# Input projection of the two mixers in groups of up to 512 columns, and the second pair of MLA heads set ahead of the compressed keys

## The chip, the cores and the metric

The kernel runs on one core of one Trainium2 chip. The metric is the device time of one execution in microseconds (us); the median of three runs stands for the kernel. TensorE (PE) multiplies into eight PSUM banks, VectorE (DVE) and ScalarE (ACT) read the banks and work on SBUF, GpSimd (POOL) works on SBUF only, and SyncE (SP) issues the loads of the weights. Each engine works through its own instructions in a fixed order.

## The reference, cut to what matters

The program is two transformer blocks one after the other. The first block has two layers, and in each layer a mixer stands between two feed-forward parts:

```python
for l in range(DEPTH):                                   # DEPTH = 2, T = 256 tokens, D = 1024
    x = x + 0.5 * swiglu(rmsnorm(x, ffn1_norm[l]), ...)
    h = rmsnorm(x, mix_norm[l]) @ w_in[l]                # 1024 -> 2290 columns
    h_a, h_b, h_c = jnp.split(h, [A_COLS, A_COLS + B_COLS], axis=-1)
    o_a = mla_mixer(h_a, ...)                            # 6 heads
    o_b = nsa_mixer(h_b, ...)                            # 6 heads, each with compressed keys and a window
    o_c = diff_mixer(h_c, ...)                           # 4 heads, two score matrices each
    x = x + jnp.concatenate([o_a, o_b, o_c], axis=-1) @ w_out[l]
    x = x + 0.5 * swiglu(rmsnorm(x, ffn2_norm[l]), ...)
```

The change touches the product with `w_in` and the order of the heads after it. The rest of the first block and the whole second block (a convolution and state-space part, then a mixture of experts) stay as they are.

## The kernel before

Weights come from memory in units of 1 MB, 128 rows by 2048 fp32 numbers, in four buffers called `st`. A helper (`split`, lines 154 to 169) splits each unit in two halves: ACT writes the rounded high part `wh` (L166), DVE the rest `wl` (L167), six buffers of each. Every product of the dense parts is three matmuls: high by high, high by low, low by high. All matmuls are issued by one helper (L98), so the tile names tell them apart.

The mixer (`_mixer`) first makes h. Its tile is called `win` in the trace. The stationary operand is the normalized input (`xhl`, 128 rows by 128 tokens), the moving operand the weight columns. Nine groups of 242 or 256 columns are made, each group in one PSUM bank whose two halves hold the two blocks of 128 tokens: 8 pieces of the inner dimension, 2 blocks of tokens and 3 products are 48 matmuls for a group, 432 for a layer. ACT then copies a group out with the norm's factor into `hA` (MLA), `hQ` and `hV` (NSA), `hC` and `hW` (differential heads).

The order of the work is one string, `ORDER`. In it `w` and digits are the groups, `mp`, `np` and `dp` prepare the three kinds of heads, `m0` to `m5`, `n0` to `n5` and `d0` to `d3` are the heads, `df` finishes the differential ones:

```python
ORDER = "w01 w5 w2 mp m0 m1 w8 w3 w4 w6 np w7 dp m2 m3 d0 d1 n0 n1 d2 d3 n2 n3 n4 n5 m4 df m5"
```

A scheduler takes the string as an order of precedence and fills what would be waits with later work that is ready; the order on each engine is then fixed. PSUM tags of the mixer are `S` (3 banks, scores and some preparation), `T` (2, transposes), `O` (1, outputs of head pairs) and `W` (2, projection and the output product).

A head runs like this: scores on PE (`S`), row maxima on DVE (`mx`, L730), exponentials on ACT (`P`, L734), scaling of P by DVE and POOL (L744), transposes of P on PE (`ptp`), copies of them by ACT or DVE (`PT`), and for each pair of heads the product with the values on PE (`opair`), copied out by ACT and DVE (`ohl`).

Compressed keys (`nsa_prepare`, step `np`) are a chain through three engines. PE transposes parts of `hQ` and `hV` (`kvc`, L781 and L782). ACT and DVE copy them in turn into `Z` (L788, four copies). DVE adds the position terms (`blk`, L794, four times). PE multiplies the result by the weights `phi` (`h`, 16 products). ACT and DVE apply the activation, and PE makes the keys and values (`kcmp`, `vcmp`). PE also transposes queries and keys there (`qtb`, `ktb`), and the step `dp` those of the differential heads (`qct`, `kct`).

At the end of the mixer the output product (`wo`) adds 192 matmuls of 256 columns for a layer. It needs the heads' outputs one after another, and its first products are spread among the last heads.

Of the kernel before, what the change touches and what calls it, by code (L numbers as in the profile page):

```python
# [22 lines left out]
KD = 8  # L23
# [13 lines left out]

LOW = {k: "pp" for k in ["b3", "x0", "x1", "x2", "x3"]}
LOW.update({k: "vp" for k in ["h3", "g2"]})
ORDER = "w01 w5 w2 mp m0 m1 w8 w3 w4 w6 np w7 dp m2 m3 d0 d1 n0 n1 d2 d3 n2 n3 n4 n5 m4 df m5"  # L40


class Block:
# [125 lines left out]
            out.append(hl)  # L169
        return out  # L170

    def cols(self, w, *segs):

        wv = w.rearrange("(k p) c -> p k c", p=128)
        out, c = [], 0
        for a, b in segs:
            out.append((c, wv[:, :, a:b]))
            c += b - a
        return self.load(out, wv.shape[1], c)
# [344 lines left out]
    def _mixer(self, l, xops, after):  # L524
        nc, a, ap, tr = self.nc, self.a, self.ap, self.nc.tensor.transpose
        xh, xl, _ = xops
        ident = self.ident
        w_in = a["w_in"][l]
        ACT = lambda o, i, **k: nc.scalar.activation(o, i, AF.Copy, **k)

        def tok(name, n, tag=None, bufs=1):
            return ap.tile([128, 2, n], F32, name=name, tag=tag or name, bufs=bufs)

        hA, hQ, hV, hC, hW = tok("hA", 352), tok("hQ", 768), tok("hV", 402), tok("hC", 512), tok("hW", 256)
        oh, ol, _ = self.pair("ohl")
        B0, C0 = 352, 1522
        q0, kc0, vc0, ks0, vs0, kw0, vw0 = [B0 + c for c in (0, 384, 512, 640, 768, 896, 1024)]
        groups = [
            ([(0, 256)], [(hA, 0, 0, 256)]),
            ([(256, 352), (vw0, C0)], [(hA, 256, 0, 96), (hV, 256, 96, 146)]),  # L540
            ([(q0, q0 + 256)], [(hQ, (0, 3), 0, 192), (hQ, 64, 192, 64)]),
            ([(q0 + 256, vc0)], [(hQ, (192, 2), 0, 128), (hQ, 384, 128, 128)]),
            ([(ks0, vs0), (kw0, vw0)], [(hQ, 512, 0, 256)]),
            ([(vc0, ks0), (vs0, kw0)], [(hV, 0, 0, 256)]),
            ([(C0, C0 + 256)], [(hC, 0, 0, 256)]),
            ([(C0 + 256, C0 + 512)], [(hC, 256, 0, 256)]),
            ([(C0 + 512, C0 + 768)], [(hW, 0, 0, 256)]),
        ]
        units = {}

        def fetch(i):
            if i < len(groups):
                units[i] = self.cols(w_in, *groups[i][0])


        small = {}
# [20 lines left out]

        steps = ORDER.split()
        queue = []
        for step in steps:  # L580
            if step[0] == "w":
                for c in step[1:]:
                    queue.append(lambda i=int(c): units.update({i: self.cols(w_in, *groups[i][0])}))
            elif step == "mp":
                queue.append(fetch_u)
            elif step == "np":
                queue.append(fetch_phi)
# [10 lines left out]
        r = self.inv_rms(pss[:, 0:2], 2)  # L598

        tags = list("WWSS")  # L600

        def w_in_groups(ids):

            ws = [self.split(units[i], "k") for i in ids]
            ps = [self.bank(tags.pop(0) if tags else "W", "win") for _ in ids]
            for k0 in range(KD):
                for k, i, t in ([(k0, i, t) for i in range(len(ids)) for t in range(2)] if len(ids) > 1 else
                                [(k, 0, k0) for k in range(KD)] if k0 < 2 else []):
                    w, p, n = ws[i], ps[i], units[ids[i]][2]
                    o = p[:, t * 256:t * 256 + n]  # L610
                    ts = slice(t * 128, (t + 1) * 128)
                    first = t == 0 and k == 0
                    last = t == 1 and k == KD - 1
                    wh, wl = (v[:, k % 4] for v in w[k // 4])
                    self.mm(o, xh[:, k, ts], wh, first, False)
                    self.mm(o, xh[:, k, ts], wl, False, False)
                    self.mm(o, xl[:, k, ts], wh, False, last)
            for i, p in zip(ids, ps):
                for dst, d, c, m in groups[i][1]:
                    for t in range(2):  # L620
                        src = p[:, t * 256 + c:t * 256 + c + m]
                        if isinstance(d, tuple):

                            o = dst[:, t, 0:384].rearrange("p (u c) -> p u c", c=64)[:, d[0] // 64::2][:, 0:d[1]]
                            src = src.rearrange("p (u c) -> p u c", c=64)
                        else:
                            o = dst[:, t, d:d + m]
                        ACT(o, src, scale=r[:, t:t + 1])


        def mla_prepare():
# [114 lines left out]
        C0, C1 = slice(256, 384), slice(0, 256)  # L746
# [141 lines left out]
        def diff_prepare():  # L888
            for t in range(2):
                self.rope(hC[:, t].rearrange("p (h c) -> p h c", h=16)[:, :, 0:8]  # L890
                          .rearrange("p h (i f) -> p h i f", i=2), 16, 4, t)
            qC = ap.tile([128, 2, T], F32, name="qC", tag="qC")

            kC = [ap.tile([128, 4, T], F32, name="kC", tag=tag) for tag in ("kC0", "hC")]
            for k in kC:
                nc.gpsimd.memset(k, 0.0)
            p, p2 = self.bank("T", "qct"), self.bank("S", "kct")
            for c in range(2):
                for t in range(2):
# [55 lines left out]
        for step in steps:  # L955
            if step == "mp":
                mla = mla_prepare()
                fetch()
            elif step == "np":
                nsa = nsa_prepare()  # L960
                fetch()
            elif step == "dp":
                dif = diff_prepare()
            elif step == "df":
                diff_finish()
            elif step[0] == "w":
                w_in_groups([int(c) for c in step[1:]])
                for _ in step[1:]:
                    fetch()
            else:  # L970
                {"m": mla_head, "n": nsa_head, "d": diff_head}[step[0]](int(step[1]))
# [4 lines left out]
        for b in range(4):  # L976
            for j, (wh, wl) in enumerate(self.split(wo[b], "n")):
                p = self.bank("WS"[j], "wo")
# [940 lines left out]
```

## Time and profile before

| | |
|---|---|
| three runs | 1525.80, 1527.27, 1530.02 us (median 1527.27) |
| the profiled execution | 1530.64 us, its span 1528.6 us |
| busy: PE, DVE, ACT, POOL | 98%, 67%, 48%, 6% |
| mean granted TensorE clock | 0.993 |
| first layer's mixer, from its first `win` to the next `gu` on PE | 200.07 to 340.07 us |

The profile page gives shares of the whole span. What a change in the mixer is worth has to be read in the mixer's own stretches, since the engine that ends last is not the same in each. Where a timeline is shown, a row is one instruction or a run of like ones: start, duration, engine, line, operation, tiles, sizes, count, and in brackets how long the engine sat idle before it and for what. Starts on PE are given by the trace, ends are modelled, so the pace of PE is read from start to start. An fp32 matmul of the heads shows as two records; the projection's matmuls show as one.

### The profile page before, as it was taken

The numbers are of one execution on the slowest core, as the hardware profiler recorded it, in microseconds if no ns is written. First come the engines' busy times: TensorE is split into PE (matmuls) and PEld (weight loads), VectorE is DVE, ScalarE is ACT, GpSimd is POOL, SyncE is SP. The second block draws the span as 40 slices with busy tenths as digits, with TensorE's granted clock in tenths as the row PEclk, the third lists the DMA queues.
The fourth block names the chain that finished last, engine by engine and source line by source line (L and its number), as shares of the span: only waits on it lengthen the run. The fifth ranks groups of instructions, "written<-read, shape, count | busy, mean of one in ns | idle before, by whom it ended". The sixth has DMA issues, their size and how long they took to land.

```text
span 1528.6 us, 25294 instructions
## 1 busy us (share of the span) xinstructions
PE 1490.9 (98%) x9906; PEld 1252.3 (82%) x9906; DVE 1025.6 (67%) x2016; ACT 728.5 (48%) x1382; POOL 91.8 (6%) x142
## 2 busy tenths in 40 slices
PE   8999999999999999999999999999899999999996
PEld 7999998789999989999888999999799987344432
DVE  6787775868677787777577877779888875122112
ACT  6555565755455555555665655547554442001011
POOL 0000000520000000000015000000510100000000
PEclk9999999999999999999999999999999999999998
DMA  7756664116556565656530555666444578999992
GB/s 252 255 165 193 192 165 157 62 61 216 188 174 193 175 189 186 193 193 175 170 119 2 193 187 175 192 191 207 148 130 124 188 294 330 371 392 392 392 395 108
DMA packets 223559, 308.93 MB, mean 202 GB/s; under 512 B 20908, under 2 KB 167608, under 8 KB 223432
## 3 DMA queue, kind: packets, MB, share of 16 engines
q1 hardware_dynamic: 223128, 306.71, 60.2%
q8 instruction: 80, 1.31, 0.4%
q10 hardware_dynamic: 304, 0.53, 0.1%
q14 instruction: 47, 0.39, 0.1%
HBM read 306.16 MB, written 1.05 MB: 201 GB/s over the span
## 4 chain that ended last, share of the span: by engine, by line
PE 92%; DVE 5%; ACT 2%; issue 1%; DMA 0%; POOL 0%; ACTq 0%; DVEq 0%
PE gu L98 32%; PE acc L98 16%; PE proj L98 7%; PE win L98 6%; PE gate L98 4%; PE y L98 4%; PE up L98 4%; PE h L98 3%; PE wo L98 3%; PE S L98 2%; PE moe L98 1%; PE opair L98 1%; PE zp L98 1%; PE xgp L98 1%; PE ptp L696 1%; DVE wl L167 1%
## 5 line engine op out<-in xcount | busy, mean ns | idle before, releaser
L167 DVE TENSOR_TENSOR wl<-st,wh 128x1024 fp32r<-128x1024 f32 (+1 forms) x370 | 446.9, 1219 | 201.9 <-ACT wh L166 190.7
L166 ACT ACTIVATE wh<-st 128x1024 fp32r<-128x1024 f32 (+1 forms) x382 | 399.5, 1059 | 338.4 <-PE gu L98 134.6
L98 PE MATMUL gu<-xhl,wh 128*128 128x512 f32 (+1 forms) x1440 | 486.6, 391 | 3.1 <-ACT wh L166 2.2
L98 PE MATMUL gu<-xhl,wl 128*128 128x256 f32 x1408 | 381.7, 280 | 0.0
L98 PEld LDWEIGHTS gu<-xhl,wh 128*128 128x128 f32 x1440 | 267.1, 189 | 60.9 <-ACT wh L166 2.6
L98 PEld LDWEIGHTS gu<-xhl,wl 128*128 128x128 f32 x1408 | 260.7, 189 | 0.2
L98 PE MATMUL acc<-hx,wh 128*128 128x256 f32 x1408 | 252.3, 281 | 0.0
L98 PEld LDWEIGHTS acc<-hx,wh 128*128 128x128 f32 x1408 | 216.3, 188 | 1.7
L98 PE MATMUL acc<-hx,wl 128*128 128x256 f32 x704 | 196.7, 281 | 0.0
L98 PEld LDWEIGHTS acc<-hx,wl 128*128 128x128 f32 x704 | 132.6, 188 | 0.0
L98 PE MATMUL proj<-uhl,wh 128*128 128x272 f32 (+2 forms) x592 | 127.5, 306 | 4.7 <-DVE dv L1186 1.6
L98 PE MATMUL win<-wh,xhl 128*128 128x256 f32 (+1 forms) x576 | 109.9, 286 | 0.2 <-DVE xT L410 0.2
L98 PEld LDWEIGHTS proj<-uhl,wh 128*128 128x128 f32 x592 | 95.8, 191 | 9.7 <-ACT cv L1224 1.7
L98 PE MATMUL proj<-uhl,wl 128*128 128x272 f32 (+2 forms) x328 | 95.0, 290 | 0.0
L98 PEld LDWEIGHTS win<-wh,xhl 128*128 128x128 f32 x576 | 91.0, 191 | 3.8 <-issue 3.1
L98 PE MATMUL win<-wl,xhl 128*128 128x256 f32 (+1 forms) x288 | 81.9, 284 | 0.0
L394 ACT ACTIVATE hx<-up 128x512 fp32r<-128x512 f32 x44 | 27.7, 630 | 87.2 <-DVE up L393 87.2
L98 PEld LDWEIGHTS proj<-uhl,wl 128*128 128x128 f32 x328 | 62.4, 190 | 0.2
L734 ACT ACTIVATE P<-S,mx 128x256 f32<-128x256 f32 (+2 forms) x128 | 49.0, 404 | 19.0 <-DVE mx L730 4.5
L744 POOL TENSOR_SCALAR P<-P,mx 128x128 f32<-128x128 f32 (+2 forms) x88 | 53.9, 632 | 58.6 <-DVE mx L737 42.7
L1816 DVE SCALAR_TENSOR_TENSOR ys<-y,rc,ys 128x512 fp32r<-128x512 f32 x16 | 11.7, 748 | 67.0 <-ACT ys L1636 66.6
L98 PEld LDWEIGHTS win<-wl,xhl 128*128 128x128 f32 x288 | 54.9, 191 | 0.6 <-issue 0.3
(524 smaller groups left out, 2117.8 us busy)
## 6 DMA issues: line engine op xcount, KB each, us to landing
st<-ffn_wg SPq DMA_DIRECT2D x44, 1024.0 KB, 6.0
st<-ffn_wu SPq DMA_DIRECT2D x44, 1024.0 KB, 5.4
st<-ffn_wd SPq DMA_DIRECT2D x44, 1024.0 KB, 4.8
st<-w_in SPq DMA_DIRECT2D x36, 1024.0 KB, 5.4
st<-w_out SPq DMA_DIRECT2D x16, 1024.0 KB
mf<-expert_w_gate SPq DMA_DIRECT2D x25, 512.0 KB, 9.4
mf<-expert_w_down SPq DMA_DIRECT2D x21, 512.0 KB, 10.7
mf<-expert_w_up SPq DMA_DIRECT2D x18, 512.0 KB, 11.0
```

What stands on the lines that cost most here:

```text
L98: return self.nc.tensor.matmul(out, lhsT, rhs, start=start, stop=stop, skip_group_check=True)
L166: hi = self.nc.scalar.activation(hl[0], src, AF.Copy)
L167: sub = (self.nc.gpsimd if lo[i] == "p" else self.nc.vector).tensor_sub(hl[1], src, hl[0].bitcast(F32))
L394: nc.scalar.activation(hh, up, AF.Copy)
L696: tr(p[:, i * 128:(i + 1) * 128], b, ident)
L734: nc.scalar.activation(P[:, d], s[:, c], AF.Exp, bias=m[:, 0, i:i + 1], accum_out=m[:, 1, i:i + 1])
L744: (nc.gpsimd if key + str(i) in "c0 c1 c2 d0 d1 m0 w0 w1".split() else nc.vector).tensor_scalar(P[:, d], P[:, d], r[:, i:i + 1], None, op0 ...
L1816: V.scalar_tensor_tensor(yl, py[half], rc[:, 1:2], yh.bitcast(F32), op0=OP.mult, op1=OP.subtract)
```

## The change

The nine groups of up to 256 columns become four of 498 or 512 and one of 256. A wide group takes two PSUM banks, one for each block of tokens, and for each piece of the inner dimension it goes through both. Its weights come in two units of 1 MB, each with half of the inner dimension, where a unit held all of it for 256 columns. The columns are regrouped, and `ORDER` is new: `m2 m3` stand ahead of `np`, and the last group with columns of the differential heads stands between `np` and `dp`.

```diff
-ORDER = "w01 w5 w2 mp m0 m1 w8 w3 w4 w6 np w7 dp m2 m3 d0 d1 n0 n1 d2 d3 n2 n3 n4 n5 m4 df m5"
+ORDER = "w0 w1 mp m0 m1 w2 w3 m2 m3 np w4 dp d0 d1 n0 n1 d2 d3 n2 n3 n4 n5 m4 df m5"
...
-    def cols(self, w, *segs):
+    def cols(self, w, *segs, part=None):
 
         wv = w.rearrange("(k p) c -> p k c", p=128)
+        if part is not None:
+            wv = wv[:, part * 4:part * 4 + 4]
...
+            ([(0, 352), (vw0, C0)], [(hA, 0, 0, 352), (hV, 256, 352, 146)]),
+            ([(vc0, ks0), (vs0, kw0), (q0, q0 + 256)],
+             [(hV, 0, 0, 256), (hQ, (0, 3), 256, 192), (hQ, 64, 448, 64)]),
+            ([(C0 + 512, C0 + 768), (q0 + 256, vc0)],
+             [(hW, 0, 0, 256), (hQ, (192, 2), 256, 128), (hQ, 384, 384, 128)]),
+            ([(ks0, vs0), (kw0, vw0), (C0, C0 + 256)], [(hQ, 512, 0, 256), (hC, 0, 256, 256)]),
             ([(C0 + 256, C0 + 512)], [(hC, 256, 0, 256)]),
...
+            wide = n > 256
+            if wide:
+                ps = [self.bank(tags.pop(0) if tags else "W", "win") for _ in range(2)]
+                outs = [p[:, 0:n] for p in ps]
+            else:
+                p = self.bank("W", "win")
+                outs = [p[:, t * 256:t * 256 + n] for t in range(2)]
...
+            for k in range(KD):
+                wh, wl = (v[:, k % per] for v in w[k // per])
+                for t in range(2):
+                    o, ts = outs[t], slice(t * 128, (t + 1) * 128)
+                    self.mm(o, xh[:, k, ts], wh, k == 0 and (wide or t == 0), False)
                     self.mm(o, xh[:, k, ts], wl, False, False)
+                    self.mm(o, xl[:, k, ts], wh, False, k == KD - 1 and (wide or t == 1))
```

The order of the instructions changes in the two mixers alone, and in both in the same way. Three places matter.

The first is on PE, from the transposes for the compressed keys (`kvc`) on. Before:

```order
L781 MATMUL kvc<-ident,hQ 128x128
L782 MATMUL kvc<-ident,hV 128x128
L781 MATMUL kvc<-ident,hQ 128x128
L782 MATMUL kvc<-ident,hV 128x128
L816 MATMUL qtb<-ident,hQ 128x128 x4
L98 MATMUL win<-wh,xhl 128x256
```

After:

```order
L782 MATMUL kvc<-ident,hQ 128x128
L783 MATMUL kvc<-ident,hV 128x128
L782 MATMUL kvc<-ident,hQ 128x128
L783 MATMUL kvc<-ident,hV 128x128
L98 MATMUL opair<-PT,vm 64x256 x2
L98 MATMUL opair<-PT,vm 64x128 x2
L817 MATMUL qtb<-ident,hQ 128x128 x6
L98 MATMUL h_2813<-blk,phi 128x60 x8
```

Before, 48 matmuls of `win` stand between `kvc` and the products `h`, with the last two `qtb` among them; after, no `win` is left there, and the four products of the pair m2, m3 (`opair`) and all of `qtb` stand there.

The second is on DVE, around the copies into `Z` that the same chain needs. Before:

```order
L702 TENSOR_TENSOR ohl<-opair,ohl 128x256
L167 TENSOR_TENSOR wl<-st,wh 128x1024
L788 COPY Z<-kvc 64x2x128 x2
L794 TENSOR_TENSOR blk<-Z,v1b 128x8x30 x4
L167 TENSOR_TENSOR wl<-st,wh 128x1024
L518 TENSOR_TENSOR rtmp<-hC,rt 128x16x4
```

After:

```order
L767 COPY PT<-ptp 128x384
L520 TENSOR_TENSOR rtmp<-hC,rt 128x16x4
L521 TENSOR_TENSOR rtmp<-hC,rt 128x16x4
L520 TENSOR_TENSOR rtmp<-hC,rt 128x16x4
L521 TENSOR_TENSOR rtmp<-hC,rt 128x16x4
L522 TENSOR_TENSOR hC<-hC,rt 128x16x8 x2
L523 TENSOR_TENSOR hC<-hC,rtmp 128x16x8 x2
L167 TENSOR_TENSOR wl<-st,wh 128x1024
L789 COPY Z<-kvc 64x2x128
L703 TENSOR_TENSOR ohl<-opair,ohl 128x256
L789 COPY Z<-kvc 64x2x128
L795 TENSOR_TENSOR blk<-Z,v1b 128x8x30 x4
```

The rotation of the differential heads' columns (`rtmp` and `hC`, eight instructions) and one `wl` stood behind `blk`, and stand ahead of `Z` now.

The third is on PE, behind the transposes of the differential heads' keys (`kct`). Before:

```order
L902 MATMUL kct<-ident,hC 128x128 x4
L98 MATMUL S<-KT,QT 128x256
L98 MATMUL S<-KT,QT 128x128
L98 LDWEIGHTS identb
L98 MATMUL S<-masks,identb 128x256
```

After:

```order
L903 MATMUL kct<-ident,hC 128x128 x4
L98 MATMUL S<-kC,qC 128x256
L98 MATMUL S<-kC,qC 128x128
L98 LDWEIGHTS identb
L98 MATMUL S<-masks,identb 128x256
```

The scores of m2 and m3 (`KT`, `QT`) are gone from here; they stand between the fourth and the fifth group now, and what follows `kct` at once are the scores of d0 (`kC`, `qC`).

## Rows read from the trace of the kernel before

**Rows 1.** Page, the chain that ended last: share of the span by engine.

```profile
PE 92%; DVE 5%; ACT 2%; issue 1%; DMA 0%; POOL 0%; ACTq 0%; DVEq 0%
```

**Rows 2.** Windows: length, busy PE, PEld, DVE, ACT, POOL; clock, DMA, GB/s.

```profile
260.00:267.10 7.10, 7.10 (x62) 7.10 (x62) 5.05 (x10) 4.24 (x8) 0.00 (x0) 1.00 0.50 166
267.10:276.70 9.60, 7.54 (x64) 6.53 (x63) 7.92 (x22) 5.19 (x17) 1.48 (x2) 1.00 0.57 186
276.70:308.50 31.80, 31.38 (x223) 25.62 (x223) 29.58 (x132) 25.18 (x120) 21.01 (x35) 1.00 0.07 23
308.50:340.10 31.60, 31.60 (x265) 28.06 (x264) 19.16 (x51) 14.58 (x29) 5.28 (x9) 1.00 0.14 44
...
779.50:790.20 10.70, 9.19 (x64) 7.87 (x62) 7.79 (x22) 5.18 (x17) 1.48 (x2) 0.84 0.63 203
...
1086.00:1088.00 2.00, 2.00 (x12) 2.00 (x12) 2.00 (x2) 0.28 (x2) 1.98 (x1) 0.57 0.91 318
```

**Rows 3.** Groups of instructions by line: the projection's matmuls, both layers.

```profile
L98 PE MATMUL win<-wh,xhl 128*128 128x256 f32 (+1 forms) x576 | 109.9, 286 | 0.2 <-DVE xT L410 0.2
```

**Rows 4.** Timeline of PE: `win`, every third matmul of a run.

```profile
213.34 0.28 PE L98 MATMUL win<-wl,xhl 128*128 128x256 f32 x1
...
213.70 0.28 PE L98 MATMUL win<-wl,xhl 128*128 128x256 f32 x1
```

**Rows 5.** Timeline of PE, second block: matmuls of 512 columns.

```profile
1235.56 1.52 PE L98 MATMUL h<-wh,vhl 128*128 128x512 f32 x6
1236.92 0.62 PE L98 MATMUL h<-wl,vhl 128*128 128x512 f32 x2
```

**Rows 6.** Timeline of PE, first layer: compressed keys to the first scores.

```profile
260.62 0.27 PE L782 MATMUL kvc<-ident,hV 128*128 128x128 f32 x1
260.73 0.60 PE L816 MATMUL qtb<-ident,hQ 128*128 128x128 f32 x4
261.09 0.36 PE L98 MATMUL win<-wh,xhl 128*128 128x256 f32 x1
...
267.13 3.67 PE L98 MATMUL h<-blk,phi 128*128 128x60 f32 x32
...
273.98 0.82 PE L98 MATMUL S<-KT,QT 96*128 96x256 f32 x4
...
274.74 0.82 PE L98 MATMUL S<-KT,QT 96*128 96x256 f32 x4
...
276.70 0.48 PE L98 MATMUL S<-kC,qC 128*128 128x256 f32 x1 [1.03 <-ACT P L734]
```

**Rows 7.** Timelines of DVE, first layer: the chain's steps, rotation, one split.

```profile
262.32 1.23 DVE L167 TENSOR_TENSOR wl<-st,wh 128x1024 fp32r<-128x1024 f32 x1 [1.54 <-ACT wh L166]
263.57 0.42 DVE L788 COPY Z<-kvc 64x256 f32<-64x256 f32 x1
...
264.89 2.20 DVE L794 TENSOR_TENSOR blk<-Z,v1b 128x240 f32<-128x240 f32 x4
...
268.15 0.26 DVE L518 TENSOR_TENSOR rtmp<-hC,rt 128x64 f32<-128x64 f32 x1
...
269.49 0.47 DVE L521 TENSOR_TENSOR hC<-hC,rtmp 128x128 f32<-128x128 f32 x2
```

**Rows 8.** Timeline of ACT, first layer: copies of the last columns and `kC`.

```profile
267.32 0.84 ACT L529 ACTIVATE hC<-win,rr 128x256 f32<-128x256 f32 x2
...
274.18 0.36 ACT L907 COPY kC<-kct 32x256 f32<-32x256 f32 x1 [0.32 <-PE kct L902]
```

**Rows 9.** Timeline of DVE, first layer: work for m2, m3 among later heads.

```profile
276.98 0.35 DVE L744 TENSOR_SCALAR P<-P,mx 128x256 f32<-128x256 f32 x1
...
280.62 0.55 DVE L766 COPY PT<-ptp 128x384 f32<-128x384 f32 x1
...
283.60 0.40 DVE L702 TENSOR_TENSOR ohl<-opair,ohl 128x256 fp32r<-128x256 f32 x1
```

**Rows 10.** Timeline of PE, second block: a long wait for DVE.

```profile
1085.77 0.49 PE L98 MATMUL proj<-uhl,wh 128*128 128x272 f32 x2 [1.61 <-DVE dv L1186]
```

More of the change, by code (lines that the diff above doesn't have):

```diff
@@ L538, in _mixer @@
         groups = [
[L539 to L545, printed above, removed]
+            ([(0, 352), (vw0, C0)], [(hA, 0, 0, 352), (hV, 256, 352, 146)]),
[4 more added lines that the diff above has]
+            ([(ks0, vs0), (kw0, vw0), (C0, C0 + 256)], [(hQ, 512, 0, 256), (hC, 0, 256, 256)]),
             ([(C0 + 256, C0 + 512)], [(hC, 256, 0, 256)]),
-            ([(C0 + 512, C0 + 768)], [(hW, 0, 0, 256)]),
         ]
         units = {}
-        def fetch(i):
-            if i < len(groups):
-                units[i] = self.cols(w_in, *groups[i][0])
         small = {}
@@ L581, in _mixer @@
             if step[0] == "w":
-                for c in step[1:]:
-                    queue.append(lambda i=int(c): units.update({i: self.cols(w_in, *groups[i][0])}))
+                i = int(step[1])
+                n = sum(e - b for b, e in groups[i][0])
+                for part in range(2) if n > 256 else [None]:
+                    queue.append(lambda i=i, part=part: units.setdefault(i, []).append(
+                        self.cols(w_in, *groups[i][0], part=part)))
             elif step == "mp":
@@ L600, in _mixer @@
         tags = list("WWSS")
[L602 to L615, printed above, removed]
-                    self.mm(o, xh[:, k, ts], wl, False, False)
[L617 to L628, printed above, removed]
@@ new lines, in w_in_group @@
+        def w_in_group(i):
+            w = [piece for u in units[i] for piece in self.split(u, "k")]
+            n = units[i][0][2]
+            wide = n > 256
[5 more added lines that the diff above has]
+                outs = [p[:, t * 256:t * 256 + n] for t in range(2)]
+            per = KD // len(w)
+            for k in range(KD):
[3 more added lines that the diff above has]
+                    self.mm(o, xh[:, k, ts], wh, k == 0 and (wide or t == 0), False)
+                    self.mm(o, xh[:, k, ts], wl, False, False)
+                    self.mm(o, xl[:, k, ts], wh, False, k == KD - 1 and (wide or t == 1))
+            for dst, d, c, m in groups[i][1]:
+                for t in range(2):
+                    src = outs[t][:, c:c + m]
+                    if isinstance(d, tuple):
+                        o = dst[:, t, 0:384].rearrange("p (u c) -> p u c", c=64)[:, d[0] // 64::2][:, 0:d[1]]
+                        src = src.rearrange("p (u c) -> p u c", c=64)
+                    else:
+                        o = dst[:, t, d:d + m]
+                    ACT(o, src, scale=r[:, t:t + 1])
@@ L966, in _mixer @@
             elif step[0] == "w":
-                w_in_groups([int(c) for c in step[1:]])
-                for _ in step[1:]:
+                w_in_group(int(step[1]))
+                for _ in units[int(step[1])]:
                     fetch()
```

## The prediction

> **What bounds the kernel now.** I read the chain of work first: PE holds 92% of it and DVE 5% [rows 1]. So a saved matmul is worth its full pace as long as PE doesn't wait, and what is to be found is where it waits. Then the stretches of the first layer's mixer [rows 2]. Up to 267.1 us PE is busy without a gap, on `win`. From 267.1 to 276.7, where the compressed keys are finished, PE is busy for 7.54 of 9.60 us: this is the one stretch with real gaps. From 276.7 to 308.5 the heads run, and DVE works 29.58 of 31.80 us (93%). PE shows 31.38 there, but with ends that are modelled, and ACT and POOL have room, so I take DVE as the limit of the heads' stretch, with PE close behind. From 308.5 on PE alone is full again, on the output product.
>
> The chain of the compressed keys is the second thing to see. `kvc` begins just ahead of 260.62, `h` follows at 267.13 [rows 6]. In between DVE makes one `wl`, the `Z` copies and `blk`: from 262.32 to 264.89 + 2.20 = 267.09 [rows 7]. PE doesn't feel these 6.4 us, because `win` runs under them, from 261.09 on. That cover is what the new order takes away.
>
> **Wide matmuls.** A run of three `win` matmuls of 256 columns takes 213.70 - 213.34 = 0.36 us from start to start [rows 4], 0.120 each; the group's mean of 286 ns [rows 3] is a modelled length and not the pace. No `win` of 512 columns is in this trace. The nearest are the `h` matmuls of the second block: six in 1236.92 - 1235.56 = 1.36 us [rows 5], 0.227 each. A layer changes 384 of 256 columns for 192 of about 512: 384 x 0.120 = 46.1 against 192 x 0.2267 = 43.5 us, which saves 2.55 us. The group of 242 columns among the old ones and the one of 498 among the new nearly cancel. Bounds: 0.5 and 3 us, the upper one if the 498-column group runs by its columns.
>
> The Trainium skill, "TensorE: Matmul & The Clock Gate", section "Back-to-back issue gap", gives N / 2.4 + 2.5 ns for an isolated matmul on the full clock; as an estimate, that is 109 ns at 256 columns and 216 at 512, so that a pair would save only 2.6 ns. By that rule 192 pairs save 0.5 us a layer, and the sum below would end 4 us higher. The trace disagrees, with 120 and 227 ns.
>
> **What moves ahead of and behind the last `win`.** I call its end E (267.13 before). Scores of m2 and m3 go ahead of it: 274.74 - 273.98 = 0.76 us a head [rows 6], 1.52 for two, and one set of three transposes, about 0.33 (a transpose takes 0.11, as the step from 260.62 to 260.73). `kvc` (four, 0.44) and `qtb` (six, 0.09 each by 261.09 - 260.73 over four, 0.54) go behind it. E comes at -2.55 + 1.52 + 0.33 - 0.98 = -1.7 us. The banks could add something: a wide group needs two, and they are free only when ACT has read the group before. Between the groups the order has scores and transposes of some 2 us, and two such reads take 0.84 us [rows 8], so I put nothing here, with a bound of 1 us either way.
>
> **From E to the first scores of d0.** Before: 276.70 - 267.13 = 9.57 us [rows 6]. After, step by step. ACT reads the last group, 0.84 us with 0.1 of handing over [rows 8], to E + 0.95. DVE's order is fixed and has the rotation ahead of `Z`: it waits for that read and takes 268.15 to 269.49 + 0.47, 1.8 us [rows 7], to E + 2.75. Then come `wl`, `Z` and `blk`, with the start of `h` in before as 267.13 - 262.32 = 4.81 us [rows 6, 7]: E + 7.55. PE has by then only transposes, `kvc`, `qtb` and four `opair`, some 2.5 us, so it stands still for about 5 us. From `h` to the end of `kct` before took 273.98 - 267.13 = 6.85 us [rows 6]. The scores of d0 then need copies of `kct` into `kC`, the first of which ended 0.56 us behind it [rows 8]; with the first one or two I put 0.45 here, for 7.3. The other copies of that stretch, on DVE, are as many as before, and one `wl` of 1.2 us less stands among them, but PE's `h` covers it. Sum: 7.55 + 7.3 = 14.8, 5.2 us more than before. Bounds: +2.4 if rotation and `wl` cost nothing and `kvc` (0.8), `Z` (1.3), `blk` (2.2) and handing over (0.4) remain; +6.5 if `wl` has to wait for its `wh` as it did before (1.54 us of idle in front of it [rows 7]). I stay at 5.2, since each of its steps has a row and the order leaves no room for the low end.
>
> **The heads' stretch.** DVE no longer has the rest of m2 and m3 in it: two scalings of 0.35, a copy of 0.55 and an `ohl` of 0.40 [rows 9], and two reciprocals that I estimate at 0.15 each, about the pace of a short `rtmp` [rows 7]. Together 1.95 us of 29.58. If DVE is the limit all of it is gained; bounds 0.9, if PE or the chain scores, maximum, exponential takes over at once, and 3.25, if the maxima of m2 and m3 and their PE work help as well. In the last stretch nothing changes, since PE is full of `wo` there.
>
> **The clock.** In the second layer the same stretch took 10.70 us with a granted clock of 0.84, in the first 9.60 with 1.00 [rows 2]: a low clock costs 1.1 us. Behind a wait of 1.61 us in the second block [rows 10] the clock shows 0.57 from 1086 to 1088 [rows 2]. A standstill of 5 us in each layer should bring the fall from the full level of 2.4 GHz in the first layer as well; the second pays already. I add 1.1 us for one more, with bounds of 0 and 5 (two falls, or longer ones, in each layer).
>
> **The sum.** A layer: -1.7 + 5.2 - 1.95 = about +1.5; rounded down for the gaps within today's 9.57 us (2.06 in all) that new fillers may take, +1.4. Two layers +2.8, and the clock 1.1: +3.9 us. The profiled execution took 1530.64 us, 0.2% above the median of 1527.27, so against it the sum is 1534.5, and against the median **1531.2 us**.
>
> **Rivals.** *The order hides the chain after all, and the kernel gets faster.* If `Z` is not held up by the rotation, the stall costs 2.4 a layer; with a relief of 3.25 the layer is at -1.7 + 2.4 - 3.25 = -2.55, both at -5.1, and the clock doesn't fall once more: 1522.2. For it speaks that DVE has idle time between E and the first scores and that its share of 93% is the highest in the mixer [rows 2]. Against it speaks the order on DVE, in which eight rotation instructions and a `wl` stand ahead of `Z`. It decides from a stall under about 3 us.
>
> *The clock makes it clearly slower.* If the standstill sends the clock to its level of 1.2 GHz while `h`, `ktb` and `kct` run (3.67 us for `h` alone [rows 6]), and again behind the wait at `kct`, these some 5 us of work take up to twice as long. At 2 us more in each layer, and a relief of only 0.9 because the late start of d0 leaves the heads waiting for one another, the layers come to 2 x (-1.7 + 5.2 - 0.9) = +5.2, with the clock's 4 to +9.2: 1536.5. For it speaks that a wait of 1.61 us was enough once [rows 10]. Against it: other waits of about a microsecond, as 1.03 ahead of d0 [rows 6], left the clock at 1.00. It decides from a standstill that lasts well beyond 1.6 us.
>
> *The wide groups don't do what they are for.* If the pace were the skill page's, the time is 3.9 + 4.1 = +8.0, 1535.3. The section is the one named above. The two paces in rows 4 and 5 speak against it; only that no 512-column `win` has been seen keeps it alive. The same would come of a wide group that waits 1 us for its second bank twice a layer.
>
> **How the numbers follow.** The forecast with its neighbours 0.54, the fast rival 0.25, the clock rival 0.17, the pace 0.04. A difference below 0.3% (4.6 us) is about what a measurement of this kernel can't tell from none. The forecast's own range is 1527 to 1534.5, by stalls from 4 to 6 us and a clock of 0 to 2; it lies on both sides of the upper mark of 1531.85, a little more below it than above: 0.32 within and 0.21 slower, with 0.01 faster. The fast rival ends between 1519 and 1525: 0.18 faster, 0.07 within. Clock and pace: 0.18 slower, 0.03 within. Together 0.20 faster (rounded up by 0.01), 0.42 within, 0.38 slower. The range of 8 in 10 runs from 1522.5 to 1537, with a tenth on each side.
>
> **What would show it.** Right: `win` of about 512 columns at 0.227 us from start to start; a gap on PE of 4 to 6 us ahead of `h` in both layers, ended by DVE's `blk`; S of d0 about 14.8 us behind the last `win`; a clock below 1.00 behind it in both layers; the heads' stretch about 2 us shorter. Wrong: a gap below 3 us, `Z` ahead of the rotation in time, a heads' stretch that is as long as before (then PE or the scores' chain was its limit), or gaps between the wide groups ended by ACT.

## The result and the profile after

The changed kernel takes 1542.56 us in the median of four executions (1539.01 to 1544.81), the kernel before 1528.45. The ratio is 1.0087, 95% interval 1.0072 to 1.0102 (that of the two medians is 1.0092): slower by 13 to 14 us, outside the stated range and more than three times what was forecast. The profiled execution, 1539.01 us with a span of 1537.1, is the shortest of the four.

Stretches of the changed kernel, in the columns of [rows 2]: from the last `win` to `h`, from `h` to the first scores of d0, from there to the last scores, and the output product; then the first two of the second layer:

```profile
266.68:273.64 6.96, 3.04 (x23) 1.77 (x21) 6.30 (x17) 3.98 (x9) 0.00 (x0) 1.00 0.25 70
273.64:284.65 11.01, 10.06 (x53) 8.91 (x53) 2.35 (x8) 1.90 (x7) 0.92 (x2) 0.54 0.39 126
284.65:315.28 30.63, 30.57 (x208) 25.63 (x209) 28.33 (x130) 24.91 (x115) 20.58 (x34) 0.94 0.03 9
315.28:346.82 31.54, 31.54 (x265) 28.06 (x263) 18.50 (x48) 14.39 (x29) 5.15 (x8) 1.00 0.15 44
785.70:792.67 6.97, 3.04 (x24) 1.78 (x22) 6.32 (x17) 3.98 (x9) 0.00 (x0) 1.00 0.25 68
792.67:803.85 11.18, 10.24 (x52) 9.09 (x52) 2.33 (x8) 1.90 (x7) 0.91 (x2) 0.53 0.41 125
```

In the first of these PE works 3.04 of 6.96 us, where before `h` stood right behind `win`. In the second the granted clock is 0.54, which means that PE ran at 1.2 GHz nearly all the time; DVE and ACT work some 2 us each of 11 and PE shows 10.06, so PE sets nearly all of that stretch. The timeline of PE in the first layer has the standstill ahead of `h` in brackets, and the scores of d0 behind it:

```profile
273.64 0.32 PE L98 MATMUL h<-blk,phi 128*128 128x60 f32 x1 [3.24 <-DVE blk L795]
...
284.65 0.80 PE L98 MATMUL S<-kC,qC 128*128 128x256 f32 x1 [0.45 <-ACT kC L908]
```

Both layers have the same 3.24 us. Laid side by side from start to start, in us:

| | before | after | difference |
|---|---|---|---|
| first layer: first `win` to behind the last | 67.06 | 66.38 | -0.68 |
| last `win` to d0 | 9.57 | 17.97 | +8.40 |
| d0 to the last scores | 31.73 | 30.58 | -1.15 |
| last scores to the next `gu` | 31.64 | 31.59 | -0.05 |
| second layer: the same four | 66.55, 10.69, 31.97, 31.63 | 65.93, 18.15, 30.52, 31.59 | -0.62, +7.46, -1.45, -0.04 |

The two mixers cost 6.52 + 5.35 = 11.9 us. The span grew by only 8.5, because the second block was 3.6 us shorter in this one execution. There the kernel before has a low clock behind a wait [rows 2, 10]; at the same place, 12 us later by the clock of the trace, the changed kernel has the wait (PE busy 0.38 of 2 us) and full clock behind it:

```profile
1096.00:1098.00 2.00, 0.38 (x5) 0.29 (x4) 1.73 (x7) 1.66 (x4) 2.00 (x2) 1.00 0.71 182
1098.00:1100.00 2.00, 2.00 (x16) 2.00 (x17) 2.00 (x1) 0.49 (x2) 2.00 (x1) 1.00 0.96 338
```

That place is worth only some 0.4 us: the distance of the two traces goes from 12.18 to 11.79 us there. The other 3.3 us lie 200 us later, around the routing of the tokens to the experts, where the distance goes from 11.80 to 8.51 us. The same 34 matmul records run there at a granted clock of 0.64 in the kernel before and at 1.00 in the changed one:

```profile
1282.80:1292.40 9.60, 9.60 (x34) 6.25 (x33) 6.73 (x39) 1.62 (x4) 0.00 (x0) 0.64 1.04 401
1294.60:1300.94 6.34, 6.34 (x34) 4.23 (x33) 6.30 (x37) 1.63 (x4) 0.00 (x0) 1.00 1.03 404
```

The change touches neither place.

The other three executions took 3 to 6 us more, and the mixers' 11.9 us, though from one execution of each kernel, is the better figure for the change than the profiled span.

### The profile page after: what moved, and what is told of

Its sections match the earlier page's. It is cut to its first block, busy times and chain, and to the rows that moved or that the text cites. A ratio compares the mean times of both kernels' runs of the same rounds, so it can differ in the third digit from the quotient of the medians.

```text
span 1537.1 us, 24555 instructions
## 1 busy us (share of the span) xinstructions
PE 1492.5 (97%) x9522; PEld 1236.8 (80%) x9522; DVE 1023.0 (67%) x2016; ACT 729.9 (47%) x1378; POOL 92.4 (6%) x142
## 3 DMA queue, kind: packets, MB, share of 16 engines
HBM read 306.16 MB, written 1.05 MB: 200 GB/s over the span
## 4 chain that ended last, share of the span: by engine, by line
PE 93%; DVE 5%; ACT 1%; DMA 1%; issue 0%; SPq 0%; ACTq 0%; DVEq 0%
PE gu L98 32%; PE acc L98 16%; PE proj L98 7%; PE win L98 7%; PE gate L98 4%; PE h L98 4%; PE y L98 4%; PE up L98 4%; PE S L98 3%; PE wo L98 3%; PE ptp L697 1%; PE opair L98 1%; PE zp L98 1%; PE moe L98 1%; PE xgp L98 1%; PE py L98 1%
## 5 line engine op out<-in xcount | busy, mean ns | idle before, releaser
L167 DVE TENSOR_TENSOR wl<-st,wh 128x1024 fp32r<-128x1024 f32 (+2 forms) x370 | 447.3, 1220 | 202.9 <-ACT wh L166 196.5
L166 ACT ACTIVATE wh<-st 128x1024 fp32r<-128x1024 f32 (+2 forms) x382 | 399.7, 1059 | 334.0 <-PE gu L98 134.1
L98 PE MATMUL win<-wh,xhl 128*128 128x512 f32 (+2 forms) x320 | 94.8, 375 | 0.2 <-DVE xT L412 0.2
L98 PEld LDWEIGHTS win<-wh,xhl 128*128 128x128 f32 x320 | 57.9, 189 | 12.5 <-issue 1.9
L98 PE MATMUL win<-wl,xhl 128*128 128x512 f32 (+2 forms) x160 | 59.5, 372 | 0.0
L735 ACT ACTIVATE P<-S,mx 128x256 f32<-128x256 f32 (+2 forms) x128 | 48.9, 396 | 11.9 <-PE ptp L697 2.8
L167 POOL TENSOR_TENSOR wl<-st,wh 128x1024 fp32r<-128x1024 f32 x12 | 28.8, 2411 | 349.9 <-DVE z L1126 251.2
```

The costliest lines, as they stand in the source:

```text
L98: return self.nc.tensor.matmul(out, lhsT, rhs, start=start, stop=stop, skip_group_check=True)
L166: hi = self.nc.scalar.activation(hl[0], src, AF.Copy)
L167: sub = (self.nc.gpsimd if lo[i] == "p" else self.nc.vector).tensor_sub(hl[1], src, hl[0].bitcast(F32))
L735: nc.scalar.activation(P[:, d], s[:, c], AF.Exp, bias=m[:, 0, i:i + 1], accum_out=m[:, 1, i:i + 1])
```

## The experiments

The theory was that the order costs: no `win` stands over the chain `kvc`, `Z`, `blk` any more, PE stands still, and the clock falls behind it. The first rival was that the wide groups cost by themselves. Mixer times are both layers together, from the first `win` to the next `gu`: 280.84 us before, 292.71 in the changed kernel.

**Width and order apart.** The old sequence with the wide groups, which is one line against the changed kernel:

```diff
-ORDER = "w0 w1 mp m0 m1 w2 w3 m2 m3 np w4 dp d0 d1 n0 n1 d2 d3 n2 n3 n4 n5 m4 df m5"
+ORDER = "w0 w1 mp m0 m1 w2 w3 np w4 dp m2 m3 d0 d1 n0 n1 d2 d3 n2 n3 n4 n5 m4 df m5"
```

> The wide groups with the sequence of before: the compressed keys (np) ahead of the fifth group, m2 and m3 behind the differential heads' preparation. Sixteen of the fifth group's matmuls stand between the first kvc and h again. Theory (the lost cover and the clock behind it cost everything): the standstill ahead of h falls from 3.2 us to under 2, the low clock behind it gets shorter or goes away, and both mixers together, from the first win to the next gu, take 281 us (+-3) as before, not 291; ratio to before 0.998 to 1.004. Rival (the wide groups themselves cost, through their pairs of banks and the halves of their weights): 287 to 291 us, ratio 1.005 to 1.009.

and the narrow groups with the new place of m2 and m3, against the kernel before:

```diff
-ORDER = "w01 w5 w2 mp m0 m1 w8 w3 w4 w6 np w7 dp m2 m3 d0 d1 n0 n1 d2 d3 n2 n3 n4 n5 m4 df m5"
+ORDER = "w01 w5 w2 mp m0 m1 w8 w3 w4 w6 m2 m3 np w7 dp d0 d1 n0 n1 d2 d3 n2 n3 n4 n5 m4 df m5"
```

> The groups of 256 columns of before, with m2 and m3 ahead of the compressed keys alone. All of win then stands ahead of kvc, as in the changed kernel. Theory (the order costs, not the width): a standstill of about 3 us ahead of h, a granted clock of 0.5 for more than 10 us behind it in both layers, both mixers together 290 to 295 us where before has 281; ratio 1.006 to 1.012. Rival (the width costs): 280 to 284 us, ratio 0.998 to 1.003.

Measured: the narrow groups in the new order 1.0117 (1.0101 to 1.0132), mixers 298.3 us. The wide groups in the old order 1.0071 (1.0057 to 1.0084), mixers 291.2 us. The timeline of PE at `h` and then the stretch from `h` to d0, of the narrow kernel:

```profile
274.91 0.32 PE L98 MATMUL h<-blk,phi 128*128 128x60 f32 x1 [3.23 <-DVE blk L794]
```

```profile
274.91:286.49 11.58, 10.46 (x53) 9.20 (x53) 2.26 (x8) 1.90 (x7) 0.92 (x2) 0.52 0.37 122
```

The same two of the wide one:

```profile
268.42 0.43 PE L98 MATMUL h<-blk,phi 128*128 128x60 f32 x2 [2.30 <-DVE blk L795]
```

```profile
268.42:281.22 12.80, 11.88 (x62) 10.23 (x62) 7.17 (x21) 3.56 (x14) 1.48 (x2) 0.60 0.52 164
```

The narrow kernel settles that the order costs, without any wide group. With the new order the wide groups even save 5.6 us of mixer time. The wide one looked like the rival at first: the old sequence of steps, and yet 0.7% slower. But its trace shows the same fault, a standstill of 2.30 us, where under 2 had been expected, and a clock of 0.60 behind it. The old string does not bring the old cover: with 512 columns in the fourth group, the last key columns are ready later, `kvc` begins 62.4 us behind the first `win` and not 60.2, and 16 `win` matmuls are left behind it instead of 48. So these two runs alone could not clear the width; a kernel with wide groups and the full cover had to.

**Width with the cover.** Three wide groups, and the last 768 columns in three narrow ones:

```diff
-ORDER = "w0 w1 mp m0 m1 w2 w3 m2 m3 np w4 dp d0 d1 n0 n1 d2 d3 n2 n3 n4 n5 m4 df m5"
+ORDER = "w0 w1 mp m0 m1 w2 w3 w4 np w5 dp m2 m3 d0 d1 n0 n1 d2 d3 n2 n3 n4 n5 m4 df m5"
...
-            ([(ks0, vs0), (kw0, vw0), (C0, C0 + 256)], [(hQ, 512, 0, 256), (hC, 0, 256, 256)]),
+            ([(ks0, vs0), (kw0, vw0)], [(hQ, 512, 0, 256)]),
+            ([(C0, C0 + 256)], [(hC, 0, 0, 256)]),
```

> Three wide groups as in the changed kernel and three of 256 columns behind them (keys, then the two of hC), with the sequence of before for the heads: kvc stands 48 win matmuls ahead of h again, and all 16 h stand together. Theory (a wide group saves what its matmuls save, as long as the chain to h stays under win): no standstill ahead of h, last win about 2 us nearer to the first than in before (288 narrow for 144 wide matmuls: 34.6 against 32.6 us), from the last win to d0 9.6 to 10.7 us as in before, both mixers together 277 us where before has 281; ratio to before 0.996 to 0.999. Rival (the pairs of banks and the half units of the wide groups give the saving back somewhere else, in the heads or as waits between groups): 281 to 284 us, ratio 1.000 to 1.003.

Measured: 0.9989 (0.9980 to 0.9999), median 1526.99 us, mixers 277.5 us, 3.35 less than before. The theory's mixer time came out to half a microsecond; the ratio lies at the weak end of what was expected. `kvc` ends 7.4 us ahead of `h`, and `h` follows the last `win` without a gap (timeline of PE, then the stretches from `h` to d0 and of the heads):

```profile
258.49 0.27 PE L784 MATMUL kvc<-ident,hV 128*128 128x128 f32 x1
...
265.82 0.28 PE L98 MATMUL win<-wh,xhl 128*128 128x256 f32 x1
265.94 3.67 PE L98 MATMUL h<-blk,phi 128*128 128x60 f32 x32
```

```profile
265.94:275.52 9.58, 7.52 (x65) 6.51 (x63) 7.13 (x22) 5.09 (x16) 0.95 (x1) 1.00 0.52 158
275.52:307.26 31.74, 31.30 (x221) 25.60 (x222) 29.45 (x131) 25.11 (x120) 20.92 (x35) 1.00 0.07 21
```

Both stretches are those of the kernel before [rows 2], at full clock. The gain lies ahead of the last `win` (1.05 and 0.98 us) and in the second layer's clock, which did not fall here (9.57 us from `h` to d0 against 10.69). That second part, some 1.3 us with the heads, rests on one execution of each kernel; the ratio stands for 1.7 us in all, the two medians differ by 2.9, and the interval ends just below 1.

Four wide groups with the keys' columns gathered in the third, so that `np` can go ahead of the fourth:

```diff
-            ([(C0 + 512, C0 + 768), (q0 + 256, vc0)],
-             [(hW, 0, 0, 256), (hQ, (192, 2), 256, 128), (hQ, 384, 384, 128)]),
-            ([(ks0, vs0), (kw0, vw0), (C0, C0 + 256)], [(hQ, 512, 0, 256), (hC, 0, 256, 256)]),
+            ([(ks0, vs0), (kw0, vw0), (q0 + 256, vc0)],
+             [(hQ, 512, 0, 256), (hQ, (192, 2), 256, 128), (hQ, 384, 384, 128)]),
+            ([(C0 + 512, C0 + 768), (C0, C0 + 256)], [(hW, 0, 0, 256), (hC, 0, 256, 256)]),
...
-ORDER = "w0 w1 mp m0 m1 w2 w3 m2 m3 np w4 dp d0 d1 n0 n1 d2 d3 n2 n3 n4 n5 m4 df m5"
+ORDER = "w0 w1 mp m0 m1 w2 np w3 w4 dp m2 m3 d0 d1 n0 n1 d2 d3 n2 n3 n4 n5 m4 df m5"
```

> Four wide groups and one of 256, but with the last columns of the keys in the third group and those of hC and hW in the fourth, and the heads in the sequence of before. 22 matmuls of 256 columns stand between kvc and h, about 3.5 us with the transposes there, against a chain of 4.5 to 5 us: a standstill of 1 to 1.5 us is left. Theory (the cost goes with the standstill, and the clock falls behind it only when it is longer than some 2 us): last win 2.5 us earlier than before, h 1 us behind, both mixers together 277 to 281 us; ratio 0.997 to 1.000. Rival (a standstill of 1 us is already followed by the low clock): 283 to 287 us, ratio 1.001 to 1.005.

Measured: 1.0004 (0.9995 to 1.0014), mixers 279.7 us, which is the theory's time. 22 `win` matmuls cover the chain, all but 0.80 us of it, and the clock stays (timeline of PE at `h`, and the stretch from there to d0):

```profile
267.10 0.43 PE L98 MATMUL h<-blk,phi 128*128 128x60 f32 x2 [0.80 <-DVE blk L795]
```

```profile
267.10:276.59 9.49, 7.49 (x62) 6.65 (x62) 7.24 (x22) 4.23 (x15) 1.48 (x2) 1.00 0.54 169
```

The two kernels together clear the width: wide groups cost nothing of their own where the chain has cover, and save about 1 us in a layer.

**What the clock costs.** PE work that nobody reads, put into the standstill of the changed kernel (26, 8 or 16 matmuls of 256 columns):

```diff
-                    tr(o, hQ[:, t, h * 128:(h + 1) * 128], ident)
+                    self.last_q = tr(o, hQ[:, t, h * 128:(h + 1) * 128], ident)
...
+            fill = self.bank("W", "fill")
+            with self.behind(self.last_q.ins):
+                for i in range(26):
+                    self.mm(fill[:, 0:256], xh[:, i % KD, 0:128], xh[:, i % KD, 0:256], True, True)
```

> The changed kernel with 26 extra matmuls of 256 columns in each mixer, between the last qtb and h, whose results nobody reads. They fill the standstill and take 3.1 us at full clock. Theory (what went beyond the forecast is the clock, which falls because PE stands still): the clock stays at 1.00 behind h, the time from h to the first scores of d0 falls from 11.0 to 7.5 us, both mixers together from 291 to about 283 us; ratio to before 1.000 to 1.004. Rival (the clock falls for another reason, or the stretch from h to the scores is bound by DVE and ACT and not by the clock): still 11 us from h to d0, 290 us or more, ratio 1.008 or more.

Measured: 1.0073 (1.0060 to 1.0086), mixers 291.4 us. By the ratio the rival won; by the stretches it did not. From `h` to d0 and the heads, first and second layer:

```profile
274.35:283.56 9.21, 7.20 (x52) 6.04 (x53) 2.43 (x8) 1.90 (x7) 0.91 (x2) 0.79 0.53 174
283.56:318.99 35.43, 33.53 (x227) 27.01 (x228) 31.02 (x143) 25.86 (x120) 21.99 (x38) 0.96 0.01 2
...
793.75:801.73 7.98, 5.97 (x53) 5.24 (x53) 2.43 (x8) 1.84 (x7) 0.92 (x2) 1.00 0.53 172
801.73:833.40 31.67, 30.89 (x207) 25.47 (x208) 28.74 (x126) 24.40 (x114) 20.38 (x34) 0.95 0.03 9
```

In the second layer the clock is at 1.00 and the stretch takes 7.98 us, where the changed kernel takes 11.18 at 0.53 with the same work: 3.2 us are the clock's alone. In the first layer the clock fell even so, later and for less: 0.79, behind a wait of 1.56 us for `h` on DVE. The same wait in the second layer left it at 1.00 (timeline of PE, first and second layer):

```profile
280.09 0.40 PE L98 MATMUL kcmp<-h,w 64*64 64x15 f32 x4 [1.56 <-DVE h L803]
...
799.49 0.29 PE L98 MATMUL kcmp<-h,w 64*64 64x15 f32 x4 [1.56 <-DVE h L803]
```

What was won in the first layer was lost in its heads, 35.43 us against 30.63, of which the last stretch gives back 2.6 (29.03 us against 31.59): the scheduler had put DVE's work of the heads in another order. The ratio is spoiled by that, the stretch is not.

Eight matmuls leave the order on all engines as it was, sixteen change DVE's a little:

> The changed kernel, every engine's sequence unchanged, with 8 extra matmuls of 256 columns in each mixer between qtb and h (1 us in all at full clock), whose results nobody reads. The standstill ahead of h falls from 3.24 to 2.3 us, h starts at the same time. Theory (the clock falls for any standstill of 2 us or more): the clock is lost as now, 14 us at 0.5 in each layer, ratio 1.007 to 1.010. Rival (the loss shrinks with each us that PE works): 12 us from h to d0 fall to 9, ratio 1.003 to 1.006.

> The changed kernel with 16 extra matmuls of 256 columns in each mixer between qtb and h (1.9 us); DVE takes the heads' maxima and scalings in a slightly other order. The standstill ahead of h falls to 1.3 us. Theory (between 0.8 us, where the clock held, and 2.3 us, where it fell, lies the length that lets it fall): if it holds here, 8 us from h to d0 and a ratio of 1.001 to 1.005; if it falls, 11 us and 1.007 to 1.010.

Measured: with 8, a standstill of 2.29 us, 1.0074 (1.0054 to 1.0094), mixers 293.5 us; with 16, a standstill of 1.34 us, 1.0076 (1.0051 to 1.0101), mixers 292.4 us. From `h` to d0, first of the one and then of the other:

```profile
273.27:284.67 11.40, 10.46 (x52) 9.31 (x52) 2.34 (x8) 1.90 (x7) 0.91 (x2) 0.52 0.37 126
```

```profile
274.55:284.56 10.01, 9.07 (x52) 7.92 (x52) 2.33 (x8) 1.90 (x7) 0.91 (x2) 0.60 0.42 138
```

The clock fell in both, so a standstill shorter by 1 to 2 us did not buy the time back, as the theory had it for 8. But of six executions of the kernel with 16, five took 1541.4 to 1545.4 us at a mean clock of 0.985 to 0.987, and one took 1531.5 us at 0.997. It is the same program, and what differs in the record is the clock. Of the 11.6 us between that one and the median of the other five, some may not belong to the mixers: executions of the kernel before at 0.997 or 0.998 took about 1526 us, those at 0.992 to 0.995 about 1530. That leaves an estimate of some 7 to 8 us for the two mixers. The stretches from `h` to d0 hold 6.2 of that in the changed kernel (11.01 and 11.18 against 7.98), and the low clock runs on behind them. The fast execution has no trace, so where it kept its clock isn't shown.

**What holds `Z` back.** The forecast put the rotation of `hC` on the path. Held behind `blk`:

```diff
-                    nc.vector.tensor_add(blk[:, half * 8:half * 8 + 8, 2 * i:2 * i + 2], src, pe)
+                    self.blk_done = nc.vector.tensor_add(blk[:, half * 8:half * 8 + 8, 2 * i:2 * i + 2], src, pe).ins
...
+            with self.behind(self.blk_done):
+                for t in range(2):
+                    self.rope(hC[:, t].rearrange("p (h c) -> p h c", h=16)[:, :, 0:8]
+                              .rearrange("p h (i f) -> p h i f", i=2), 16, 4, t)
```

> The changed kernel with the rotation of hC held until the last blk is made, so that only one wl stands ahead of Z on DVE. Theory (each instruction ahead of Z lengthens the standstill by its own time): the standstill ahead of h falls from 3.24 to about 1.4 us. If its length also decides whether the clock falls, the clock holds and both mixers together lose 2 x (1.8 + 3.5), to 280 to 283 us, ratio 0.998 to 1.003; if 1.4 us is enough for the fall, 2 x 1.8 is gained, 287 us, ratio 1.006. Rival (the rotation then holds up qct and kct, so that the scores of d0 start as late as now): 290 us, ratio 1.008.

Measured: 1.0113 (1.0098 to 1.0127), mixers 296.6 us, worse than the theory and the rival. The standstill went from 3.24 to 2.92 us only. The ratio is spoiled as in the filled kernel: DVE's order in the heads is another, and they took 35.89 us in the first layer. DVE in the changed kernel, and then in this one, whose trace has the last `win` 0.69 us earlier:

```profile
267.68 0.27 DVE L520 TENSOR_TENSOR rtmp<-hC,rt 128x64 f32<-128x64 f32 x1
...
269.03 0.47 DVE L523 TENSOR_TENSOR hC<-hC,rtmp 128x128 f32<-128x128 f32 x2
269.44 1.21 DVE L167 TENSOR_TENSOR wl<-st,wh 128x1024 fp32r<-128x1024 f32 x1
270.67 0.42 DVE L789 COPY Z<-kvc 64x256 f32<-64x256 f32 x1
...
272.04 2.04 DVE L795 TENSOR_TENSOR blk<-Z,v1b 128x240 f32<-128x240 f32 x4
```

```profile
268.14 1.23 DVE L167 TENSOR_TENSOR wl<-st,wh 128x1024 fp32r<-128x1024 f32 x1 [1.07 <-ACT wh L166]
269.40 0.42 DVE L789 COPY Z<-kvc 64x256 f32<-64x256 f32 x1
```

With the rotation gone, DVE waits 1.07 us for ACT's `wh` in its place. Counted from the last `win`, the first `Z` on DVE comes 0.58 us earlier and `h` 0.32, since DVE's second `Z` then waits 0.29 us for ACT's. The rotation had filled a wait, and only a third of a microsecond of it was on the path. ACT, in the changed kernel, shows what stands ahead there:

```profile
267.01 0.85 ACT L531 ACTIVATE hC<-win,rr 128x256 f32<-128x256 f32 x2
267.74 1.07 ACT L166 ACTIVATE wh<-st 128x1024 fp32r<-128x1024 f32 x1
268.68 0.36 ACT L789 COPY Z<-kvc 64x256 f32<-64x256 f32 x1
```

A split of the output product's weights, `wh` on ACT and then `wl` on DVE, stands ahead of both engines' first `Z`. Holding the later splits behind the last copy into `kw` (`self.keys`):

```diff
-            for j, (wh, wl) in enumerate(self.split(wo[b], "n")):
+            with ExitStack() as held:
+                if b:
+                    held.enter_context(self.behind(self.keys.ins))
+                parts = self.split(wo[b], "n")
+            for j, (wh, wl) in enumerate(parts):
```

> The changed kernel with the splits of the output product's units after the first held behind the copies into ks and kw; on DVE no wl stands between the rotation and Z any more, on ACT one wh still stands ahead of Z. Theory (not the rotation but the wl, which waits for its wh on ACT, holds Z on DVE): the standstill ahead of h falls by 1.2 us, from 3.24 to about 2 us; the clock still falls, so both mixers together lose some 2.5 us against the changed kernel, 290 us, ratio 1.006 to 1.008. Rival (ACT alone holds Z): the standstill stays above 2.9 us.

Measured: the standstill fell by 1.20 us, as the theory had it, but the time went the other way, 1.0145 (1.0128 to 1.0162), mixers 299.8 us:

```profile
272.52 0.47 PE L98 MATMUL h<-blk,phi 128*128 128x60 f32 x1 [2.04 <-DVE blk L795]
...
283.59 0.40 PE L98 MATMUL kcmp<-h,w 64*64 64x15 f32 x4 [3.24 <-DVE h L803]
```

The held splits, four of 1.2 us, landed on DVE right ahead of the activation `h` that `kcmp` needs, and made a second standstill of 3.24 us. The clock was low for even longer: from `h` to d0 it took 14.55 and 15.98 us. The run shows the step and is no gain.

**Is the early pair worth anything?** Three wide and three narrow groups, with m2 and m3 ahead of the keys and 20 `win` matmuls under the chain, against the kernel with the pair behind:

```diff
-ORDER = "w0 w1 mp m0 m1 w2 w3 w4 np w5 dp m2 m3 d0 d1 n0 n1 d2 d3 n2 n3 n4 n5 m4 df m5"
+ORDER = "w0 w1 mp m0 m1 w2 w3 m2 m3 w4 np w5 dp d0 d1 n0 n1 d2 d3 n2 n3 n4 n5 m4 df m5"
```

> The kernel with three wide and three narrow groups, and m2 and m3 ahead of the compressed keys, as in the changed kernel, but with 20 win matmuls, qtb and opair between kvc and h. Theory (taking m2 and m3 out of the heads is worth 1.2 to 2 us a layer, and the changed kernel paid for it only with its cover): a standstill of about 1 us ahead of h, the clock above 0.9, the stretch from d0 to the last scores 30 to 30.6 us in both layers against 31.7 with m2 and m3 behind, both mixers together 277 to 279 us; ratio 0.996 to 0.999. Rival (a standstill of 1 us and a chain that is some 1.5 us later take the gain, with or without the clock): 281 us or more, ratio 1.000 to 1.004.

Measured: 1.0007 (0.9996 to 1.0018), mixers 281.7 us, 4.2 more than with the pair behind; the rival holds. From `h` to d0 and the heads, both layers:

```profile
271.48:278.84 7.36, 5.96 (x52) 5.28 (x52) 5.20 (x17) 2.89 (x9) 0.86 (x2) 1.00 0.39 125
278.84:309.25 30.41, 29.20 (x207) 24.48 (x208) 28.64 (x126) 24.38 (x114) 20.44 (x34) 1.00 0.13 41
783.27:791.77 8.50, 7.10 (x52) 5.99 (x52) 5.20 (x17) 2.95 (x9) 0.86 (x2) 0.81 0.50 156
791.77:824.03 32.26, 31.12 (x208) 25.56 (x209) 28.56 (x126) 24.64 (x114) 20.45 (x34) 0.94 0.08 25
```

At full clock, in the first layer, the heads are 31.74 - 30.41 = 1.33 us shorter; that is what the pair is worth there. From `h` to d0 it takes 2.22 less, since the pair's scores are gone from there. But its scores, transposes and products put the last `win` 2.97 us later than in the kernel with the pair behind, and `h` starts 1.22 us behind it, 0.83 of them a standstill, so the layer loses 0.6 us in all. In the second layer the clock fell too, behind a wait of 0.95 us ahead of `kcmp` that had left it at 1.00 in the first (0.96), and the relief is gone.

## Why the prediction was wrong

The direction and the mechanism were those of the forecast: cover lost, standstill, low clock. The sum was +3.9 us; the mixers took +11.9. Of the 8.0 us between them, the work behind the standstill took 5.4 more than forecast, the last `win` came 2.1 later, the heads gave 1.3 less, the way from the last `win` to `h` took 1.2 less, and the rest, 0.4, is rounding. By its steps:

**The clock** is the step that failed most. It had 1.1 us for one more fall, beside the 1.1 that the second layer paid before, 2.2 in all. In both layers the stretch from `h` to d0 took 11.01 and 11.18 us where 7.3 had been forecast: 7.6 us. The filled kernel has the changed kernel's work there and takes 7.98 at full clock, by which 6.2 of the 7.6 us are the clock's and 1.4 are waits that the 7.3 left out (the kernel with the pair ahead, with other work on DVE, takes 7.36). The mistake was to price a fall by what one had cost in the second layer before, 0.84 over 10.7 us [rows 2]. Behind the standstill of the first layer the clock stayed at 0.5 for all but the first microsecond of the stretch and for over 3 us of the heads:

```profile
274.50:288.20 13.70, 12.70 (x58) 10.68 (x57) 4.36 (x13) 3.64 (x13) 1.34 (x2) 0.50 0.29 93
```

The clock rival had the place right, even the word "twice", and priced it at 4 us; its 1536.5 was still too low, and the step's own upper bound of 5 us was reached by these two stretches alone (6.2 less the 1.1 paid before).

**Wide matmuls** had the pace right. From start to start, three of 512 columns take 0.68 us in the changed kernel, 0.227 each, and the `win` rows together take 2.4 us less in each layer (2.55 forecast):

```profile
255.60 0.39 PE L98 MATMUL win<-wl,xhl 128*128 128x512 f32 x1
256.28 0.39 PE L98 MATMUL win<-wl,xhl 128*128 128x512 f32 x1
```

The Trainium skill, "TensorE: Matmul & The Clock Gate", section "Back-to-back issue gap", gives N / 2.4 + 2.5 ns for an isolated matmul on the full clock, 216 at 512 columns, by which a pair saves 2.5 ns and not 2.6. The `win` rows here, at 227, do not bear it out.

But **the last `win`** came only 0.68 and 0.62 us earlier, not 1.7. What moves past it was priced well (+1.87 - 0.93 by the rows against +1.85 - 0.98), so about 0.8 us of the saving went elsewhere. The rows of `qp`, MLA's first products, show a part of it, in the kernel before and then after:

```profile
228.77 3.66 PE L98 MATMUL qp<-wm,cqT 128*128 128x288 f32 x12
```

```profile
230.70 4.05 PE L98 MATMUL qp<-wm,cqT 128*128 128x288 f32 x12
```

The same twelve records take 0.39 us more with wide groups around them, in every kernel that has them. They come in another order. Before, the loads of the stationary operand (PEld) with 128 rows and with 64 rows alternate by four, four, two and two; after, by twos throughout. The first of the other kind starts 0.39 us after PEld's last one ended each time:

```profile
228.66 0.79 PEld L98 LDWEIGHTS qp<-wm,cqT 128*128 128x128 f32 x4
229.83 0.78 PEld L98 LDWEIGHTS qp<-wm,cqT 64*128 64x128 f32 x4 [0.39 <-ACT wh L166]
231.00 0.30 PEld L98 LDWEIGHTS qp<-wm,cqT 128*128 128x128 f32 x2 [0.39 <-PE qp L98]
```

```profile
231.27 0.29 PEld L98 LDWEIGHTS qp<-wm,cqT 64*128 64x128 f32 x2 [0.39 <-issue]
231.95 0.30 PEld L98 LDWEIGHTS qp<-wm,cqT 128*128 128x128 f32 x2 [0.39 <-issue]
```

From start to start a run of four takes 1.17 us and two of two take 2 x 0.68 = 1.36, so the two runs that are split account for about all of the 0.39. By the same count `vp`, MLA's values, takes 0.50 more and `qtp` 0.1 less, which is the rest. Where `vp` ends and `win` begins is rough, since two `win` stand among its records before, and why it takes more isn't settled.

**From the last `win` to `h`** 7.55 us were forecast and 6.96 measured. The rotation gives way to `wl` 2.76 us behind the last `win` (2.75 forecast), and from `wl` to `h` it takes 4.20 instead of 4.81, a stretch in which DVE had waited 0.43 us for ACT's `Z` before:

```profile
264.43 0.43 DVE L788 COPY Z<-kvc 64x256 f32<-64x256 f32 x1 [0.43 <-ACT Z L788]
```

The sum is good, but not its reason. The rotation's 1.8 us, which the forecast called sure because of the order on DVE, lay for the most part under a wait for ACT; without it `h` came 0.32 us earlier. The reading of `hC` and the split on ACT and DVE were the path. An order tells which instruction comes first, not which of them is waited for; the trace of before had shown that very `wl` with 1.54 us of waiting for its `wh` [rows 7], and the forecast used it as an upper bound (+6.5, where 5.2 + 1.54 makes +6.7) instead of asking what else it would hide.

**The heads** got 1.15 and 1.45 us shorter, 1.33 at full clock, not 1.95. DVE's work there fell from 29.58 [rows 2] to 28.33 us, about as much as the stretch, so the pair's share was smaller than the rows counted for it. That fits DVE as the limit and doesn't show it: between the two kernels with three wide groups, at full clock, the stretch fell by 1.33 us, DVE's work by 0.81 and PE's by 2.10, and no run tells the two apart.

**The tail** took no part, as said (31.6 us in all four).

**The range and chances.** The fast rival, with 0.25, rested on the chain shrinking to its bare steps; no step of it came true. Too much of the chance stood there and too little on the clock falling in both layers for as long as the engine needed to finish the chain.

## What to carry to other kernels

Before moving work away from in front of a chain that crosses engines, count what is left under that chain in the new order, in the engine's own instructions; the saving of the moved work is small against the chain's length. Price an uncovered chain on TensorE twice, once for the standstill and once for the work behind it at half the clock, until the trace shows the clock back. Here the wider tiles paid only where the last narrow pieces stayed to cover the chain: three wide groups and three narrow ones beat the changed kernel clearly and the one before by a hair (0.9989, up to 0.9999), four wide ones with part of that cover came out level with the kernel before (1.0004).

## What was not expected of the hardware

How long the clock stays low, and that it is not the same each time. Behind standstills of 2.3 to 3.2 us it was 0.5 through ten microseconds and more in which PE shows 10 of 11 us as busy, since at half the clock the same work fills the time. Behind 0.80 us it held. At waits of 0.9 to 1.0 us it held in some stretches and fell in others ([rows 2], second layer of before; the second layer of the kernel with the pair ahead), and a wait of 1.56 us in the filled kernel was followed by a fall in one layer and by none in the other. With 1.34 us it fell in the profiled execution, and by the mean clock it did not in one of six of the same program. What decides in such a case isn't settled by these runs.
